# A hybrid SSD/attention block on one core: the store of the gated forms ten k steps later, the first gate/up pair in the common order, the first ring loads at their slots' release

## The chip, the cores and the metric

The kernel runs on one core of one Trainium2 chip. The metric is the device time of one execution in microseconds (us). The time before is 2273.95 us, the median of three runs (2269.09, 2274.33 and 2273.95).

## The reference

One transformer-like block on a sequence of 512 tokens, 2048 channels wide, all in fp32:

```python
u = rmsnorm(h, attn_norm_w)
z, xbc, dt_raw, q, kc, vc, ks, vs, kw, vw, gate_raw = jnp.split(u @ w_in, split_at, axis=-1)
y_ssd = ssd_mixer(z, xbc, dt_raw, conv_w, conv_b, dt_bias, a_log, d_skip, ssd_norm_w)
y_att = nsa_mixer(q, kc, vc, ks, vs, kw, vw, gate_raw, ...)
h = h + jnp.concatenate([y_ssd, y_att], axis=-1) @ w_out
v = rmsnorm(h, ffn_norm_w)
h = h + (jax.nn.silu(v @ w_gate) * (v @ w_up)) @ w_down
return rmsnorm(h, final_norm_w)
```

Only the line with `w_gate`, `w_up` and `w_down` matters here. `w_gate` and `w_up` are 2048 x 5632, `w_down` is 5632 x 2048.

## The kernel before

**Products.** Every fp32 operand is split into a high and a low part that TensorE reads as fp32r. ScalarE makes the high part (`a_hi`, L122: a copy that rounds), VectorE the low part (`lo`, L125: the operand less its high part). A product is then high by high, high by low and low by high. L134 is VectorE's plain addition, L128 its multiplication by two factors, L131 its multiplication, L281 a small operation of the norm.

**Gate and up.** The columns of `w_gate` and of `w_up` are worked in 22 pairs u = 0 to 21; one side of a pair is 256 columns of `w_gate` (side 0, gate) or of `w_up` (side 1, up). Each side is a 2x2 block product made with seven products in place of eight (Winograd's form of Strassen's scheme): M1 to M7. Their weight operands are the blocks 11, 12, 22 and the sums S1 = 21 + 22 and S3 = 21 + 11. S1 and S3 are made in memory: SyncE loads the first block, then GpSimd issues a load that adds the second one to it (L1109, `Z<-in_w_gate` and `Z<-in_w_up` on GpSimd's queue). M6 uses 11 with S1 added and M3 uses 12 with 11 added; VectorE makes these two sums just before the form is made (`sums`, L134). On the data's side M1, M2 and M6 use parts of v as they are, the others use T0 to T3, which are sums of the quarters of v, split into high and low parts in six pieces (`t_piece`).

**A step** is one of the seven products for one side: 8 k steps, each with a matmul of 512 columns and one of 256 (both L1168), so a side is 56 k steps and a pair 112. Each k step ends with `sch.tick()`, which lets the pending generators (evictions, silu, forms of the gated product) count down one; `yield n` in a generator means "go on n k steps from now". The high and low parts of a step's weights are issued two to three steps ahead of it (`prep(s.i + 2)`, `form(i + 1)`).

**Order and banks.** In pairs 1 to 20 the seven steps of a side come in the order SEQ = M1, M5, M6, M2, M7, M3, M4, gate whole and then up whole. M1, M6, M7 and M4 go into one PSUM bank, M5 and M3 into a second, M2 into a third (to which M1 is copied first, so that M2 adds to it). When a step ends, its bank is evicted: M1 (L1379), M6 (L1384), M2 (L1389), M5 (L1395) and M4 (L1411) by ScalarE, M7 and M3 by VectorE, which adds to an earlier eviction. So M6's eviction must be done before M7 may write. The banks have the names `ps_g`, `ps_s` and `ps_t` in turn.

In pairs 0 and 21 the two sides alternate step by step (`both_sides`). Pair 21 follows SEQ. Pair 0 follows M1, M2, M3 of both sides and then M6, M5, M7, M4 of both; M3's two sums (11 into S1's place and 12 plus 11) are made at once, and the pieces of T0 to T3 are made ahead of its steps 1 to 6.

**The gated product.** After M4 of up, `silu(gate) * up` of the pair stands in one buffer. `g_forms` (L1433 to L1455) makes its seven data forms for the down projection with their high and low parts: waits of 10, 4, 4 and 6 k steps lie between its pieces, and the last piece is the store of all seven (1.79 MB, L1454, `g_d<-A`) from ScalarE's queue. 24 k steps after M4 of up is the last k step of M6 of the next pair's gate side. ScalarE carries out its instructions in order, so what stands behind the store waits until the store is issued; the store is issued when the last low part is there.

**Down projection.** It walks over visits (a stretch of pairs for a block of output columns; L1172 to L1174 are its matmuls, L1524 and on its steps) and reads the stored forms through a ring of seven slots, whose memory is that of the parts of v and T0 to T3. Each slot is filled in two halves (forms 0 to 3 and 4 to 6, 1.0 MB and 0.77 MB) by `feed` (L1533 to L1553) with loads on ScalarE's queue (L1548, `u<-g_d`, `V<-g_d`, `T<-g_d`). A slot comes free when the last pair's up side is done with the step that reads it; `done[n - GRING, half]` holds that step's number for slot n. The first five early halves were issued at the third step behind the release (for slots 0 and 1 behind the release of the next slot).

The instructions are issued in the order of the program text from the first 16 steps of the output projection on; no scheduler moves them.

Of the kernel before, what the change touches and what calls it, by code (L numbers as in the profile page):

```python
# [10 lines left out]
AF = mybir.ActivationFunctionType  # L11
ALU = mybir.AluOpType
# [13 lines left out]
GRING = 7  # L26
# [17 lines left out]
M1, M2, M3, M4, M5, M6, M7 = range(1, 8)  # L44
V_OF = {M1: 0, M2: 1, M3: 2, M5: 3, M6: 4, M7: 5, M4: 6}
SEQ = [M1, M5, M6, M2, M7, M3, M4]
# [66 lines left out]
def body(ctx, tc, xT, w_in, w_out, w_gate, w_up, w_down, w1k, w1v, cols, rows, kst, out):  # L113
# [19 lines left out]
    def add(eng, o, a, b):  # L133
        eng.tensor_tensor(o, a, b, ALU.add)  # L134
# [1228 lines left out]
    def gu_after(u, side, got):  # L1363
        both = u in (0, NP - 1)

        def after(pr):
            def ev(p):
                wv = P2["A"][:, 12:28, :].rearrange("p (b a) t -> p b (a t)", b=4)
                if both:
                    wv = wv[:, 2 * side:2 * side + 2]  # L1370
                u2, m5 = wv[:, 0 if both else 1, :], wv[:, 1 if both else 3, :]
                ct = P2["CT"].rearrange("p (s c a) t -> p s c (a t)", s=2, c=2)
                c = ct[:, side].rearrange("p a t -> p (a t)")
                g = ct[:, 0].rearrange("p a t -> p (a t)")
                c4 = c.rearrange("p (a t) -> p a t", a=4)
                if pr == M1:
                    if u:
                        got["W"] = bank()
                    act.activation(got["W"] if u else u2, p, AF.Copy)  # L1379
                elif pr == M6:  # L1380
                    if u == 0:
                        add(dve, u2, got["W"], u2)
                        add(dve, c4[:, 0], u2[:, lo_h], u2[:, hi_h])
                    act.activation(u2, p, AF.Copy)  # L1384
                elif pr == M2:
                    if u and both:
                        fold(c4[:, 0], p)
                    elif u:
                        act.activation(wv[:, 0, :], p, AF.Copy)  # L1389
                elif pr == M5:  # L1390
                    if u == 0:
                        dve.tensor_tensor(m5, p, m5, ALU.subtract)
                        add(dve, u2, p, u2)
                    else:
                        act.activation(m5, p, AF.Copy)  # L1395
                elif pr == M7:
                    add(dve, m5, p, m5)
                    if u == 0:
                        add(dve, c4[:, 1:4:2], wv[:, :, lo_h], wv[:, :, hi_h])
                elif pr == M3:  # L1400
                    if u == 0:
                        act.activation(m5, p, AF.Copy)
                    else:
                        add(dve, u2, p, u2)
                        if both:
                            add(dve, c4[:, 1:4:2], wv[:, :, lo_h], wv[:, :, hi_h])
                elif pr == M4:
                    if both:
                        fold(c4[:, 2], p)
                    else:  # L1410
                        act.activation(wv[:, 2, :], p, AF.Copy)  # L1411
                        add(dve, c4, wv[:, :, lo_h], wv[:, :, hi_h])
                    if side == 0:
                        rr = rrow[:, None, :].to_broadcast([128, 2, 512])
                        c2 = ct[:, 0]
                        mul(dve, c2, c2, rr)
                        sch.add(silu(u, g, c2, rr, 0 if both else 10))
                    else:
                        sch.run_until(("r", u))
                        mul(dve, c, c, g)  # L1420
                        sch.add(g_forms(u))
            return ev
        return after
# [9 lines left out]
    def g_forms(u):  # L1433

        ct = P2["CT"].rearrange("p (s c a) t -> p s c (a t)", s=2, c=2)
        g = ct[:, 1]
        tg = ct[:, 0].rearrange("p a t -> p (a t)").rearrange("p (a t) -> p a t", a=4)
        sg = P2["ST"][:, 0:14, :].bitcast(F32R).rearrange("p (v s) t -> p v s t", s=2)
        yield 10
        a_hi(sg[:, 0, 0, :], g[:, 0, lo_h])  # L1440
        a_hi(sg[:, 1:3, 0, :], g[:, 1, :].rearrange("p (a t) -> p a t", a=2), scale=-1.0)
        gq = g.rearrange("p c (a t) -> p (c a) t", a=2)
        dve.tensor_tensor(tg[:, 1, :], gq[:, 1, :], gq[:, 0, :], ALU.subtract)
        add(dve, tg[:, 2, :], gq[:, 1, :], gq[:, 3, :])
        add(dve, tg[:, 0, :], tg[:, 1, :], gq[:, 3, :])
        dve.tensor_tensor(tg[:, 3, :], tg[:, 0, :], gq[:, 2, :], ALU.subtract)
        yield 4
        lo(dve, sg[:, 0, 1, :], g[:, 0, lo_h], sg[:, 0, 0, :])
        neg_lo(sg[:, 1:3, 1, :], g[:, 1, :].rearrange("p (a t) -> p a t", a=2), sg[:, 1:3, 0, :])
        a_hi(sg[:, 3:7, 0, :], tg)  # L1450
        yield 4
        lo(dve, sg[:, 3:7, 1, :], tg, sg[:, 3:7, 0, :])
        yield 6
        nc.scalar.dma_start(g_d[u].rearrange("v p n -> p v n"), f(sg).rearrange("p v s t -> p v (s t)"))  # L1454
        sch.flags.add(("g", u))  # L1455

    def start_ff(n):

        def before():
            if n == 0:  # L1460
                sch.run_until(*[("oa", c) for c in range(KD)])
                P2["T"].update({i: U[:, i - 2, 8:16, :].rearrange("p k (s t) -> p k s t", s=2) for i in (2, 3)})


                v = [P2["V0"], P2["VV"][:, 0], P2["VV"][:, 1]] + [P2["T"][i] for i in range(4)]
                P2["slot"] = [v[i] for i in V_SLOT]
                P2["turn"], P2["spare"] = 0, P2["SR"]
                P2["H"] = [x.rearrange("p (k a) t -> p k (a t)", a=2) for x in
                           [P2["A"][:, i:i + 10, :] for i in range(0, 70, 10)] + [P2["Z"][:, NZ2:NZ, :]]]
            else:  # L1470
                t_piece(*[(0, 1), (1, 1), (2, 0), (2, 1), (3, 0), (3, 1)][n - 1])
        return before

    r3 = rms_stats(acc2, D, rrow, "r3", rel=True)
# [13 lines left out]
    def both_sides(u, order, seq):  # L1488
        loads.extend(qs[u, int(a[0])][a[1:]] for a in order.split())
        bk = {i: gu_banks() for i in range(2)}  # L1490
        af = {i: gu_after(u, i, bk[i][0]) for i in range(2)}
        for n, (side, p) in enumerate(seq):
            ev = af[side](p)
            if u == 0 and n in (1, 4):
                ev = step_r3(ev)
            q = qs[u, side]
            b, sums = q["form"][p]
            if u == 0 and p in (M3, M6):
                sums = [(q["11"], q["S1"]), (q["12"], q["11"])] if p == M3 else ()
            if u and n == 0:  # L1500
                before = lambda: P2.update(spare=P2["ST"][:, 14:16, :])
            else:
                before = start_ff(n) if u == 0 and n < 7 else None
            s = Step(b, v_rhs(p), bk[side][1](p), after=ev, before=before, sums=sums,
                     wide=True)
            if (u, side) == (NP - 1, 1):
                n = V_SLOT.index(V_OF[p]) - GRING
                done[n, 0] = done[n, 1] = s.i

    done = {}  # L1510
    both_sides(0, "011 111 0S1 012 112 1S1 0S3 1S3 022 122", [(i, p) for p in (M1, M2, M3) for i in range(2)] +
               [(i, p) for p in (M6, M5, M7, M4) for i in range(2)])
    for u in range(1, NP - 1):
        for side in range(2):
            add_loads(qs[u, side])
# [15 lines left out]
    later = {}  # L1531

    def feed(i):  # L1533

        for half, r in ((0, slice(0, 4)), (1, slice(4, 7))):
            while nxt["ring", half] < NP:
                n = nxt["ring", half]
                at = max(done.get((n - GRING, half), i), later.get(n, 0))
                if n < 2 and half == 0:
                    at = done.get((n + 1 - GRING, 0), i)  # L1540
                if n < 5 and half == 1:
                    at = done.get((4 - GRING, 0), i) + n // 2
                if at + 3 > i:
                    break
                if n == NP - 1:
                    sch.run_until(("g", n))
                G[n] = P2["slot"][n % GRING]
                nc.scalar.dma_start(f(G[n][:, r]).rearrange("p v s t -> p v (s t)"),  # L1548
                                    g_d[n, r].rearrange("v p n -> p v n"))
                nxt["ring", half] += 1  # L1550
        if "H0" not in P2 and len(G) > 0 and not any(az.busy):
            load_h(0)
            P2["H0"] = True  # L1553
# [352 lines left out]
```

## Time and profile before

| | before |
|---|---|
| median of three runs | 2273.95 us |
| the profiled execution | 2275.06 us |
| its span, first to last instruction | 2273.3 us |
| its mean granted TensorE clock | 0.984 of full speed |
| first pair (0) | 893.02 to 939.20, 46.18 us |
| pairs 1 to 20 | 939.20 to 1752.77, 813.57 us |
| first visit of the down projection | 1791.99 to 1815.87, 23.88 us |

The profile names an instruction by its source line, engine, operation and the buffers that it writes and reads. PE is TensorE's matmuls, PEld its weight loads (beside the matmuls), DVE is VectorE, ACT is ScalarE, POOL is GpSimd, SP is SyncE; ACTq, POOLq and SPq are the DMAs that these issue. In a timeline row the first number is the start in us from the span's start, the second the duration; "x16" means sixteen alike in a row, and the brackets hold the idle time ahead of the row with what ended it. A row of the waits gives who waited for whom, the total in us, how often and the longest. A row of the DMA issues gives size and the time from issue to landing. Helpers record under one line: every high part is L122, every low part L125.

### The profile page before, as it was taken

How to read it: one execution, taken by the hardware profiler on the slowest of the kernel's cores; microseconds unless marked ns; L12 is line 12 of the kernel's file. 1: busy time of each engine (PE TensorE's matmuls, PEld its weight loads, DVE VectorE, ACT ScalarE, POOL GpSimd, SP SyncE). 2: the span in 40 equal slices, each digit the busy share in tenths (PEclk: the TensorE clock that was granted, in tenths of full speed). 3: DMA queues.
4: the chain of work that ended last, by engine and by line, in shares of the span. 5: the costliest groups of instructions: out<-in, count | busy, mean ns of one | idle time of the engine just before them, and what ended most of it. 6: DMA issues, size and time to landing. Idle time of an engine off the chain costs nothing. (4 is left out here: it accounts for less than half of the span.)

```text
span 2273.3 us, 35008 instructions
## 1 busy us (share of the span) xinstructions
PE 2177.7 (96%) x12904; PEld 1916.4 (84%) x12904; DVE 1822.6 (80%) x2858; ACT 1187.4 (52%) x1961; POOL 426.1 (19%) x433
## 2 busy tenths in 40 slices
PE   7999999999989989999999999999999899999996
PEld 5888888888877777888888888888888899999996
DVE  7699766688888667878888788887887798988897
ACT  4564446567666544655555555555555443333453
POOL 2011224223133224000000100001000121221222
PEclk8999999999989999999999999999999999999999
DMA  5222343222413265787878878788787969796974
GB/s 176 93 70 75 128 136 103 75 85 73 137 60 125 69 223 166 227 219 219 236 211 248 219 219 236 211 249 219 219 236 212 333 236 307 189 297 180 300 190 134
DMA packets 168555, 417.17 MB, mean 184 GB/s; under 512 B 16592, under 2 KB 23520, under 8 KB 168384
## 3 DMA queue, kind: packets, MB, share of 16 engines
q1 hardware_dynamic: 99776, 252.24, 33.7%
q0 software_dynamic: 25888, 76.72, 17.2%
q10 hardware_dynamic: 42720, 85.99, 10.5%
q8 instruction: 101, 1.65, 0.3%
q14 instruction: 70, 0.57, 0.1%
HBM read 353.80 MB, written 57.41 MB: 181 GB/s over the span
## 5 line engine op out<-in xcount | busy, mean ns | idle before, releaser
L122 ACT ACTIVATE R<-Z 128x1024 fp32r<-128x1024 f32 (+4 forms) x457 | 420.8, 934 | 442.7 <-DVE Z L134 315.0
L125 DVE TENSOR_TENSOR R<-Z,R 128x1024 fp32r<-128x1024 f32 (+4 forms) x363 | 393.6, 1092 | 41.1 <-ACT R L122 30.5
L232 PE MATMUL ps_g<-u,whi 128*128 128x512 f32 x720 | 286.1, 397 | 0.2 <-DVE h L131 0.2
L234 PE MATMUL ps_g<-u,wlo 128*128 128x512 f32 x720 | 284.4, 395 | 0.0
L233 PE MATMUL ps_g<-u,whi 128*128 128x512 f32 x720 | 283.9, 394 | 0.0
L1168 PE MATMUL ps_s<-u,R 128*128 128x512 f32 (+1 forms) x1152 | 253.4, 349 | 26.8 <-ACT A L1384 26.3
L1168 PEld LDWEIGHTS ps_s<-u,R 128*128 128x128 f32 x1152 | 186.6, 188 | 60.0 <-ACT A L1384 32.9
L125 DVE TENSOR_TENSOR wlo<-wraw,whi 128x512 fp32r<-128x512 f32 x196 | 151.3, 775 | 66.0 <-ACT whi L122 65.4
L122 ACT ACTIVATE whi<-wraw 128x512 fp32r<-128x512 f32 x196 | 122.6, 626 | 134.4 <-PE ps_g L233 89.7
L234 PEld LDWEIGHTS ps_g<-u,wlo 128*128 128x128 f32 x720 | 135.6, 188 | 27.1
L232 PEld LDWEIGHTS ps_g<-u,whi 128*128 128x128 f32 x720 | 135.9, 189 | 26.0 <-DVE h L131 0.5
L233 PEld LDWEIGHTS ps_g<-u,whi 128*128 128x128 f32 x720 | 135.8, 189 | 25.4
L1168 PE MATMUL ps_t<-u,R 128*128 128x512 f32 x592 | 132.5, 350 | 0.0
L134 DVE TENSOR_TENSOR A<-ps_g,A 128x512 f32<-128x512 f32 (+1 forms) x114 | 73.9, 655 | 73.1 <-PE ps_g L1168 39.1
L1168 PE MATMUL ps_g<-u,R 128*128 128x512 f32 (+1 forms) x600 | 131.5, 348 | 0.0
L1168 PE MATMUL ps_g<-T,R 128*128 128x512 f32 (+1 forms) x584 | 126.9, 348 | 0.0
L1168 PE MATMUL ps_s<-T,R 128*128 128x512 f32 (+1 forms) x552 | 123.9, 351 | 0.0
L1172 PE MATMUL ps_g<-u,R 128*128 128x256 f32 (+1 forms) x353 | 115.1, 326 | 9.0 <-ACT R L122 7.1
L122 ACT ACTIVATE R<-A 128x1024 fp32r<-128x1024 f32 (+3 forms) x79 | 74.7, 946 | 92.3 <-DVE A L134 65.2
L1168 PE MATMUL ps_s<-V,R 128*128 128x512 f32 (+1 forms) x568 | 122.7, 347 | 0.0
L125 DVE TENSOR_TENSOR E<-Z,R 128x1024 fp32r<-128x1024 f32 x94 | 114.6, 1219 | 9.4 <-ACT R L122 6.5
L1173 PE MATMUL ps_g<-u,R 128*128 128x256 f32 (+1 forms) x353 | 114.1, 323 | 0.0
(484 smaller groups left out, 5702.8 us busy)
## 6 DMA issues: line engine op xcount, KB each, us to landing
Z<-in_w_gate SPq DMA_DIRECT2D x95, 512.0 KB, 5.5
Z<-in_w_up SPq DMA_DIRECT2D x94, 512.0 KB, 5.1
wraw<-in_w_in SPq DMA_DIRECT2D x164, 256.0 KB, 2.6
g_d<-A ACTq DMA_DIRECT2D x22, 1792.0 KB, 13.9
Z<-in_w_gate POOLq DMA_DIRECT2D x39, 512.0 KB, 5.6
Z<-in_w_up POOLq DMA_DIRECT2D x38, 512.0 KB, 7.4
Z<-in_w_down SPq DMA_DIRECT2D x58, 320.0 KB, 5.4
Z<-in_w_down SPq DMA_DIRECT2D x40, 384.0 KB, 4.1
```

The costliest lines, as they stand in the source:

```text
L122: act.activation(dst, src, AF.Copy, scale=scale)
L125: eng.tensor_tensor(dst, src, f(hi), ALU.subtract)
L134: eng.tensor_tensor(o, a, b, ALU.add)
L232: pe.matmul(p, hi_t[i][:, j, :], ah, start=(k == 0), stop=False)
L233: pe.matmul(p, hi_t[i][:, j, :], al, start=False, stop=False)
L234: pe.matmul(p, lo_t[i][:, j, :], ah, start=False, stop=(k == u.nk - 1))
L1168: pe.matmul(o, w, x, start=start, stop=(k == n - 1 and o is q), skip_group_check=not fresh[0])
L1172: pe.matmul(q, h[:, k, :], ah, start=(k == 0), stop=False)
L1173: pe.matmul(q, h[:, k, :], al, start=False, stop=False)
```

## The change

Three edits. First, the store of the seven gated forms goes from 24 to 34 k steps after M4 of up (`yield 6` to `yield 16`). Second, pair 0 takes the order SEQ like the others, with its loads, the pieces of T0 to T3 (`PIECES`) and its evictions changed to suit: M1's eviction goes to a part of the result buffer, M2's eviction adds to it, and M6 and M3 get their one sum each, as in other pairs. Third, the early halves of ring slots 0 to 4 are issued at the first step behind the release of their memory, `done + 1`; the late halves are issued as before.

```diff
@@ evictions of gate and up (gu_after)
+                p1 = c[:, 256:768]
                 if pr == M1:
                     if u:
                         got["W"] = bank()
-                    act.activation(got["W"] if u else u2, p, AF.Copy)
+                    act.activation(got["W"] if u else p1, p, AF.Copy)
                 elif pr == M6:
-                    if u == 0:
-                        add(dve, u2, got["W"], u2)
-                        add(dve, c4[:, 0], u2[:, lo_h], u2[:, hi_h])
                     act.activation(u2, p, AF.Copy)
                 elif pr == M2:
-                    if u and both:
+                    if u == 0:
+                        add(dve, p1, p, p1)
+                        add(dve, c4[:, 0], p1[:, lo_h], p1[:, hi_h])
+                    elif both:
                         fold(c4[:, 0], p)
-                    elif u:
+                    else:
                         act.activation(wv[:, 0, :], p, AF.Copy)
                 elif pr == M5:
-                    if u == 0:
-                        dve.tensor_tensor(m5, p, m5, ALU.subtract)
-                        add(dve, u2, p, u2)
-                    else:
-                        act.activation(m5, p, AF.Copy)
+                    act.activation(m5, p, AF.Copy)
                 elif pr == M7:
                     add(dve, m5, p, m5)
...
@@ g_forms
         lo(dve, sg[:, 3:7, 1, :], tg, sg[:, 3:7, 0, :])
-        yield 6
+        yield 16
         nc.scalar.dma_start(g_d[u].rearrange("v p n -> p v n"), f(sg).rearrange("p v s t -> p v (s t)"))
         sch.flags.add(("g", u))
+
+    PIECES = {1: (1, 1), 4: (2, 0), 5: (2, 1), 7: (3, 0), 9: (3, 1)}
@@ start_ff
+                t_piece(0, 1)
             else:
-                t_piece(*[(0, 1), (1, 1), (2, 0), (2, 1), (3, 0), (3, 1)][n - 1])
+                t_piece(*PIECES[n])
@@ both_sides
-            if u == 0 and p in (M3, M6):
-                sums = [(q["11"], q["S1"]), (q["12"], q["11"])] if p == M3 else ()
...
-                before = start_ff(n) if u == 0 and n < 7 else None
+                before = start_ff(n) if u == 0 and (n == 0 or n in PIECES) else None
...
-    both_sides(0, "011 111 0S1 012 112 1S1 0S3 1S3 022 122", [(i, p) for p in (M1, M2, M3) for i in range(2)] +
-               [(i, p) for p in (M6, M5, M7, M4) for i in range(2)])
+    both_sides(0, "011 111 0S1 1S1 012 112 0S3 1S3 022 122", [(i, p) for p in SEQ for i in range(2)])
@@ feed
-                at = max(done.get((n - GRING, half), i), later.get(n, 0))
-                if n < 2 and half == 0:
-                    at = done.get((n + 1 - GRING, 0), i)
-                if n < 5 and half == 1:
-                    at = done.get((4 - GRING, 0), i) + n // 2
-                if at + 3 > i:
+                at = max(done.get((n - GRING, half), i), later.get(n, 0)) + 3
+                if n < 5:
+                    at = done.get((n - GRING, 0), i) + 1 if half == 0 else done.get((4 - GRING, 0), i) + 3 + n // 2
+                if at > i:
                     break
```

The numbers of the lines behind the edits shift: the evictions of M6, M2, M5 and M1 go from L1384, L1389, L1395 and L1379 to L1382, L1390, L1392 and L1380, the store from L1454 to L1446, the ring loads from L1548 to L1538.

The first place is ScalarE's instructions in the gate side of pair 11, from the eviction of M5 on; L1384 (L1382) is the eviction of M6, L1389 (L1390) that of M2, and `R<-Z` and `R<-A` are high parts of weights. Before:

```order
L1395 ACTIVATE A<-ps_g 128x512
L122 ACTIVATE R<-A 128x1024
L1454 DMA g_d<-A 128x7x512
L1384 ACTIVATE A<-ps_s 128x512
L122 ACTIVATE R<-Z 128x1024
L1389 ACTIVATE A<-ps_t 128x512
L122 ACTIVATE R<-Z 128x1024 x3
```

and of the change:

```order
L1392 ACTIVATE A<-ps_g 128x512
L122 ACTIVATE R<-Z 128x1024
L1382 ACTIVATE A<-ps_s 128x512
L122 ACTIVATE R<-Z 128x1024
L1390 ACTIVATE A<-ps_t 128x512
L122 ACTIVATE R<-Z 128x1024
L1446 DMA g_d<-A 128x7x512
L122 ACTIVATE R<-Z 128x1024 x2
```

The store has moved from ahead of M6's eviction to behind M2's and one more high part; two high parts, of later steps, follow it.

The second place is VectorE's instructions at the start of pair 0; `T_8314` is T0, the data operand of M5, `T_8315` is T1, that of M6, `E<-Z,R` and `R<-Z,R` are low parts of weights, `rst` is the norm's. Before:

```order
L128 SCALAR_TENSOR_TENSOR T_8314<-Z,T_8314 128x4x256
L134 TENSOR_TENSOR Z<-Z 128x1024 x2
L125 TENSOR_TENSOR R<-A,R 128x1024
L281 TENSOR_SCALAR rst<-ps_m 128x4
L131 TENSOR_TENSOR rst<-rst 128x4 x2
L125 TENSOR_TENSOR T_8315<-A,T_8315 128x4x256
L134 TENSOR_TENSOR Z<-Z 128x1024
L134 TENSOR_TENSOR A<-A,Z 128x1024
L125 TENSOR_TENSOR E<-Z,R 128x1024
```

and of the change:

```order
L125 TENSOR_TENSOR u<-A,u 128x2x256
L125 TENSOR_TENSOR T_8315<-A,T_8315 128x4x256
L134 TENSOR_TENSOR Z<-Z 128x1024
L125 TENSOR_TENSOR R<-Z,R 128x1024
L281 TENSOR_SCALAR rst<-ps_m 128x4
L131 TENSOR_TENSOR rst<-rst 128x4 x2
L134 TENSOR_TENSOR Z<-Z 128x1024
L125 TENSOR_TENSOR E<-Z,R 128x1024
```

One sum now stands ahead of each low part where two stood; T1's piece comes ahead of the first sum.

The third place is ScalarE's instructions in the last pair (21), between M1's evictions and M6's; `V_8321` and `T_8314` are ring slots. Before:

```order
L1395 ACTIVATE A<-ps_t 128x512
L122 ACTIVATE R<-Z 128x1024
L1395 ACTIVATE A<-ps_g 128x512
L122 ACTIVATE R<-Z 128x1024
L1384 ACTIVATE A<-ps_s 128x512
L122 ACTIVATE R<-Z 128x1024
L1384 ACTIVATE A<-ps_g 128x512
L1548 DMA V_8321<-g_d 128x4x512
```

and of the change:

```order
L1380 ACTIVATE ps_s<-ps_g 128x512
L1538 DMA V_8321<-g_d 128x4x512
L122 ACTIVATE R<-Z 128x1024
L1392 ACTIVATE A<-ps_t 128x512
L122 ACTIVATE R<-Z 128x1024
L1392 ACTIVATE A<-ps_g 128x512
L1538 DMA T_8314<-g_d 128x4x512
L122 ACTIVATE R<-A 128x1024
L1446 DMA g_d<-A 128x7x512
L1382 ACTIVATE A<-ps_s 128x512
```

The first ring load stands right behind M1's second eviction, four steps earlier, and the second right behind M5's; the store of pair 20 stands behind both of them.

More of the change, by code (lines that the diff above doesn't have):

```diff
@@ L1378, in ev @@
                         got["W"] = bank()
-                    act.activation(got["W"] if u else u2, p, AF.Copy)
+                    act.activation(got["W"] if u else p1, p, AF.Copy)
                 elif pr == M6:
-                    if u == 0:
-                        add(dve, u2, got["W"], u2)
-                        add(dve, c4[:, 0], u2[:, lo_h], u2[:, hi_h])
                     act.activation(u2, p, AF.Copy)
                 elif pr == M2:
-                    if u and both:
+                    if u == 0:
+                        add(dve, p1, p, p1)
+                        add(dve, c4[:, 0], p1[:, lo_h], p1[:, hi_h])
+                    elif both:
                         fold(c4[:, 0], p)
-                    elif u:
+                    else:
                         act.activation(wv[:, 0, :], p, AF.Copy)
                 elif pr == M5:
-                    if u == 0:
-                        dve.tensor_tensor(m5, p, m5, ALU.subtract)
-                        add(dve, u2, p, u2)
-                    else:
-                        act.activation(m5, p, AF.Copy)
+                    act.activation(m5, p, AF.Copy)
                 elif pr == M7:
                     add(dve, m5, p, m5)
-                    if u == 0:
+                elif pr == M3:
+                    add(dve, u2, p, u2)
+                    if both:
                         add(dve, c4[:, 1:4:2], wv[:, :, lo_h], wv[:, :, hi_h])
[L1400 to L1406, printed above, removed]
                 elif pr == M4:
```

## The prediction

> **What bounds the kernel now.** The page's first section comes first: which engine is near its limit.
>
> ```profile
> PE 2177.7 (96%) x12904; PEld 1916.4 (84%) x12904; DVE 1822.6 (80%) x2858; ACT 1187.4 (52%) x1961; POOL 426.1 (19%) x433
> ```
>
> TensorE (PE) is busy for 2177.7 of 2273.3 us, so about 96 us of it are idle. No edit of this change takes a matmul away; it can only win idle time. The profiled execution took 2275.06 us (1.8 us outside the span), 1.1 us over the median of the runs (2273.95). I sum against 2275.06. About 0.3%, 6.8 us, is what a measurement can tell from no change.
>
> Second, the busy time by stage. The columns are the stretch, its length, busy us of PE, PEld, DVE, ACT and POOL, the granted clock, the DMA share and GB/s.
>
> ```profile
> 893.02:939.20 46.18, 42.56 (x238) 36.69 (x236) 39.38 (x45) 25.80 (x31) 8.71 (x9) 0.96 0.66 176
> 910.50:913.94 3.44, 3.44 (x14) 2.96 (x13) 3.44 (x4) 2.55 (x3) 0.60 (x1) 0.50 0.45 151
> 939.20:1752.77 813.57, 787.26 (x4481) 684.42 (x4480) 661.89 (x682) 448.35 (x583) 69.54 (x81) 1.00 0.80 226
> 1712.23:1733.26 21.03, 19.82 (x113) 17.11 (x112) 17.62 (x21) 11.54 (x16) 1.73 (x2) 1.00 0.76 221
> 1733.26:1752.77 19.51, 19.51 (x113) 17.10 (x112) 14.61 (x14) 11.25 (x15) 2.16 (x3) 1.00 0.80 227
> 1791.99:1815.87 23.88, 17.36 (x107) 16.71 (x106) 18.90 (x26) 8.40 (x15) 7.11 (x5) 0.79 1.02 376
> ```
>
> These are the first pair, a piece of it at half clock, pairs 1 to 20, the gate side and the up side of pair 20, and the first visit of the down projection. The two sides hold the same 113 matmul records, yet gate takes 21.03 us and up 19.51: 1.52 us are lost on every gate side.
>
> Third, what PE waited for; the columns are total, times, longest.
>
> ```profile
> PE ps_s L1168 <- ACT A L1384: 26.3, 20, 2.4
> ...
> PE ps_t L1168 <- DVE E L125: 3.1, 1, 3.1
> PE ps_s L1172 <- DMA u<-g_d: 2.9, 1, 2.9
> ...
> PE ps_g L1172 <- DMA u<-g_d: 1.8, 1, 1.8
> ```
>
> The largest wait comes 20 times, once in each pair from 1 to 20, and ends with L1384, ScalarE's (ACT's) eviction of M6. Fourth, that place in the order of time, in one pair.
>
> ```profile
> 1396.66 1.07 ACT L122 ACTIVATE R<-Z 128x1024 fp32r<-128x1024 f32 x1 [0.59 <-DVE Z L134]
> 1398.87 0.37 ACTq L1454 DMA_DIRECT2D g_d<-A  x1
> 1399.28 0.60 ACT L1384 ACTIVATE A<-ps_s 128x512 f32<-128x512 f32 x1 [1.55 <-DVE A L125]
> ...
> 1397.62 1.22 DVE L125 TENSOR_TENSOR A<-A 128x1024 fp32r<-128x1024 f32 x1
> ...
> 1395.71 2.94 PE L1168 MATMUL ps_t<-u,R 128*128 128x512 f32 x16
> 1399.93 0.51 PE L1168 MATMUL ps_s<-u,R 128*128 128x512 f32 x1 [1.28 <-ACT A L1384]
> ```
>
> M7 writes the bank that M6's eviction reads. That eviction stands behind the store of the previous pair's forms on ACT's queue, and the store waits for VectorE's (DVE's) last low part (1397.62 + 1.22 = 1398.84). So ACT stands still for 1.55 us with a finished M6 before it, and M7 starts at 1399.93.
>
> **Part one, the store (pairs 1 to 20).** Without the store ahead of it the eviction follows the form: 1396.66 + 1.07 = 1397.73, plus 0.60 is 1398.33. A side without wait has 7 steps in 19.51 us, 2.787 each, so M7 is due at 1395.71 + 2.79 = 1398.50. The eviction makes it with 0.2 us to spare. The wait should go whole, but the next one stands close.
>
> The store's 34th k step is the second of M7: it now stands behind the evictions of M6 and M2 and two forms. Its data is 10 k steps (3.5 us) old by then, so it should wait for nothing, and its 0.37 us lie in ACT's idle time (448 of 814 us busy). Behind it wait forms of M3 and M4, two steps ahead of their use. The buffer that it reads is written again only 122 k steps after M4 (a pair is 112), 88 after the new issue, 31 us; the store lands in 13.6 (below).
>
> The bound of this part is 813.57 - 40 x 19.51 = 33.2 us. Two pieces may stay. Pair 1 waits 2.4 us, 1.1 more than the others, and I leave 0.8 there. The other is the up side's second wait:
>
> ```profile
> 1073.92 0.37 ACTq L1454 DMA_DIRECT2D g_d<-A  x1
> 1075.84 0.88 POOL L1109 DMA_DIRECT2D Z<-in_w_up  x1 [10.80 <-DMA Z<-in_w_up]
> 1088.59 1.06 ACT L122 ACTIVATE R<-Z 128x1024 fp32r<-128x1024 f32 x1 [1.58 <-DMA Z<-in_w_up]
> 1094.78 0.50 PE L1168 MATMUL ps_s<-u,R 128*128 128x512 f32 x1
> ...
> ACT R L122 <- DMA Z<-in_w_up: 6.5, 9, 1.6
> ...
> Z<-in_w_up POOLq DMA_DIRECT2D x1, 512.0 KB, 5.3
> ...
> Z<-in_w_up POOLq DMA_DIRECT2D x1, 512.0 KB, 12.7
> ...
> g_d<-A ACTq DMA_DIRECT2D x1, 1792.0 KB, 13.6
> ```
>
> The accumulating load of up's S3, issued 1.9 us after the store, lands in 12.7 us; the one before it, issued at 1064 with no store beside it, takes 5.3. ACT waits for it 9 times, 6.5 us in all. At 1.58 us of waiting PE loses only 0.14 (1094.78 against M2's 1091.86 + 2.78), so about 1.4 us of delay is free. But the load is anchored ahead of the stall that goes, and its user comes 1.5 us earlier: the free margin is spent. What is left is the nine waits, 6.5 us, less what the load wins because the store starts about level with it and no longer 1.9 us ahead. From 0 to 6.5 I take 2.4. **Part one: 33.2 - 0.8 - 2.4 = 30 us** (22 to 33).
>
> The Trainium skill says in "DMA: Bandwidth & Descriptors" (Issuing engines are not separate DMA queues) that transfers of all issuing engines run on the same 16 DMA engines and interleave. By it the later store still shares them with that load, and no order of issue shields it; this speaks against the change. The rows agree (12.7 against 5.3). If no time at all is won for the load, part one is 26 us and the total 2242.
>
> **Part two, the first pair.** 46.18 us stand against 14 steps x 2.787 = 39.02, plus the norm's small matmuls, about 1.5. So 5.7 us is the most that can be won. They are these:
>
> ```profile
> 903.17 2.82 PE L1168 MATMUL ps_s<-u,R 128*128 128x256 f32 x15 [0.50 <-DVE R L125]
> ...
> 909.35 0.38 PE L1168 MATMUL ps_t<-u,E 128*128 128x256 f32 x1 [3.12 <-DVE E L125]
> ...
> 906.93 1.22 DVE L134 TENSOR_TENSOR A<-A,Z 128x1024 f32<-128x1024 f32 x1
> 908.08 1.22 DVE L125 TENSOR_TENSOR E<-Z,R 128x1024 fp32r<-128x1024 f32 x1
> ...
> 896.49 1.20 POOL L1248 TENSOR_TENSOR A<-Z,A 128x256 f32<-128x256 f32 x1
> ```
>
> 3.12 us because M3 stood third and its two sums come ahead of its low part on DVE; 0.50; and 1.7 lost at half clock (3.44 us at 0.50), soon after the 3.12 us stall.
>
> In the new order M5 is third, without a sum, and M6 fifth with one. DVE's row: T1's piece waits for the subtraction on GpSimd (POOL) at 896.49 + 1.20, then ACT's high part (1.05), and ends near 900.0; one sum and M5-up's low part end at 902.5, where M5-up is due at 893.02 + 3 x 2.787 + 0.8 = 902.2: 0.4 us late. The norm's small operations, a sum and M6's low part end near 905.8, where M6 is due at 905.4: 0.4 more. After that DVE gains on PE. Up's S1 is now the fourth load, so it lands some 10 us before use. One late us and no half clock leave 4.5; I take **4 us**. The ends are 5.7, and -3.4 if one stall brings two half-clock windows (1.7 each).
>
> The Trainium skill, "TensorE: Matmul & The Clock Gate" (What's actually happening), gives the clock a free-running window of about 3.4 us after which an idle array runs at half rate. The 3.44 us at 0.50 agree. By it two waits of 0.4 us cost no window; were the half clock due to something else, this part would be 1.7 us smaller and the total 2239.7.
>
> **Part three, the first ring loads.** The first visit takes 23.88 us, of which 2.9 and 1.8 are waits for ring slots, with a clock of 0.79. The early half of slot 0 is now issued 4 steps earlier, of slots 1 to 4 two to four; the late halves stay.
>
> ```profile
> 1752.00:1772.00 20.00, 20.00 (x115) 17.33 (x114) 16.46 (x19) 12.62 (x17) 1.73 (x2) 1.00 0.72 176
> 1772.00:1792.00 20.00, 20.00 (x117) 17.54 (x116) 15.74 (x18) 6.67 (x9) 2.37 (x2) 1.00 1.04 389
> ...
> u<-g_d ACTq DMA_DIRECT2D x1, 1024.0 KB, 13.7
> ```
>
> The DMA engines are full from 1772 on and at 0.72 before. Two early halves (2.1 MB, 5.5 us at 389 GB/s) fit into the free share, so the later ones land about 5 us earlier; the slot that PE waits for, issued at 1782.7, took 13.7. The 2.9 us should go, the 1.8 perhaps. But DVE is busy 18.90 of the 23.88, so the visit can win at most 5.0. Zero is the other end; I take **3.4**. Each new issue now stands directly behind the eviction that frees its slot, so on ACT it adds 0.37 us each, inside 6.67 busy of 20. Should ACT block there, it is the forms of M3 and M4 that come late, with two steps of lead.
>
> Sum: 2275.06 - 30 - 4 - 3.4 = **2237.7**, say 2238. The forecast's own range, from the parts' ends: 2275.06 - 33.2 - 5.7 - 5.0 = 2231, to 2275.06 - 22 - 0 - 0 = 2253.
>
> **The rivals.**
> - The weight load takes the wait's place. In the ten pairs where up's S3 is latest, M7 of the up side loses the 1.53 us that gate won: 2238 + 15 = 2253; in all twenty, 2268. For it: margin 1.4 and loss 1.5 are equal, and store and load still overlap. Against it: 11 of 20 pairs show no wait at all, and the store's head start goes.
> - M6's eviction slips past its 0.2 us, since the sum and form ahead of it depend on DVE (1.55 us of its 39 are enough): 0.5 us a pair, 20 x 0.5 = 10, so 2248.
> - The edit doesn't do what it says, and M7 waits for something beside the store. Parts two and three alone give 2275.06 - 7.4 = 2267.7. Against: the store's wait and M7's wait match to the tenth.
> - Slower: the later store and up's S3 block each other. If that load lands in 15.0 us and not 12.7 (a ring load issued at 1784 took 15.0), it is 2.3 late, its user 1.53 early, with 1.1 of margin left in a mean pair: 2.75 lost against 1.53 won, 20 x 1.2 = 24 us, less 7.4: 2292. It decides once that load lands about 1.5 us later than now.
>
> ```profile
> V<-g_d ACTq DMA_DIRECT2D x1, 768.0 KB, 15.0
> ```
>
> **How the numbers follow.** Forecast 2238: 0.62. Weight load 2253: 0.20. Eviction 2248: 0.05. No effect 2267.7: 0.05. Slower 2292: 0.04. Below 2229, where all parts reach their bounds and more: 0.04. The range 2229 to 2260 leaves out the last three and the upper tail of the second, 0.17. Faster by over 0.3% (under 2267): all but the no-effect and slower cases and 0.01 of the weight loads, 0.90; within 0.3%: 0.06; slower: 0.04.
>
> **What would show it.** Part one: no PE wait on the M6 eviction (20 now), gate sides of 19.5 us, and ACT's wait ahead of the eviction gone. Wrong would be: PE waits in the up side's M7, ACT waits for in_w_up grown past 15 us in total. Part two: from the first gate matmul to pair 1 under 43 us, no clock of 0.50 in it. Part three: no wait for g_d in the first visit, DVE as what ends the waits left. The forecast fails if the pair's mean stays above 40 us (40.7 now).

## The result and the profile after

The changed kernel takes 2249.29 us, the median of four runs (2247.54 to 2254.77), against 2274.14 for the kernel before with its four runs. The ratio is 0.9898, with a 95% interval of 0.9878 to 0.9918: some 25 us less, where 36 were forecast. The time lies in the stated range, between the forecast (2238) and the first rival, the weight load (2253), and nearer to the rival. The profiled execution, the fastest of the four, took 2247.54 us, 27.5 less than the one of before.

First the page's first section after the change (busy us of each engine, share of the span):

```profile
span 2245.7 us, 35046 instructions
...
PE 2171.9 (97%) x12904; PEld 1913.6 (85%) x12904; DVE 1814.7 (81%) x2856; ACT 1182.8 (53%) x1961; POOL 425.0 (19%) x433
```

TensorE still idles 73.8 us of the span (95.6 before). Second, the stages, in the view by windows (length, busy PE, PEld, DVE, ACT, POOL, clock, DMA share, GB/s): the first pair, the gate side of pair 1, pairs 1 to 20, the gate side and the up side of pair 17, the first visit.

```profile
893.92:934.62 40.70, 40.70 (x237) 35.45 (x236) 34.89 (x40) 22.53 (x27) 7.71 (x9) 1.00 0.66 180
934.62:957.84 23.22, 20.33 (x114) 16.95 (x112) 21.34 (x25) 14.91 (x21) 1.72 (x2) 1.00 0.73 210
934.62:1728.82 794.20, 785.78 (x4481) 684.35 (x4480) 663.12 (x684) 445.94 (x586) 69.06 (x80) 1.00 0.82 233
1570.31:1589.88 19.57, 19.57 (x113) 17.14 (x112) 17.63 (x21) 11.43 (x16) 1.73 (x2) 1.00 0.78 211
1589.88:1610.57 20.69, 19.77 (x113) 17.10 (x112) 15.45 (x15) 10.68 (x15) 1.72 (x2) 1.00 0.86 243
1768.44:1790.11 21.67, 16.05 (x106) 15.44 (x105) 19.86 (x26) 8.30 (x15) 5.88 (x4) 0.84 0.86 316
```

The gate side, 21.03 before, is down to 19.57: its stall is gone. Now it is the up side that is long, 20.69 against 19.51. Third, the waits of PE and then those of ScalarE:

```profile
PE ps_s L1168 <- ACT A L1382: 6.1, 11, 0.9
...
PE ps_g L1172 <- DMA u<-g_d: 2.8, 1, 2.8
...
PE ps_g L1168 <- DVE R L125: 1.5, 1, 1.5
...
PE ps_s L1168 <- DVE E L125: 0.8, 1, 0.8
```

```profile
ACT R L122 <- DMA Z<-in_w_up: 32.8, 20, 2.5
...
ACT R L122 <- DMA Z<-in_w_gate: 6.6, 1, 6.6
```

M7's wait for M6's eviction is down from 26.3 us to 6.1, and ten of the eleven that are left stand in up sides. ScalarE's wait for the up side's S3 load has grown from 6.5 us to 32.8. These are the two signs of being wrong that the prediction named for part one.

For the balance each side is taken from the first matmul of its M1 to the first of the next. In us, from the two profiled executions:

| stage | before | after | won |
|---|---|---|---|
| up to the first pair | 893.02 | 893.92 | -0.90 |
| pair 0 | 46.18 | 40.70 | 5.48 |
| pair 1, gate and up | 22.18 + 19.52 | 23.22 + 19.98 | -1.50 |
| 19 gate sides, pairs 2 to 20 | 400.27 | 371.36 | 28.91 |
| 19 up sides, pairs 2 to 20 | 371.60 | 379.64 | -8.04 |
| pair 21 | 39.22 | 39.62 | -0.40 |
| first visit | 23.88 | 21.67 | 2.21 |
| the rest | 457.43 | 455.59 | 1.84 |

### The profile page after: what moved, and what is told of

Read it like the earlier page. It is cut to its first block, busy times and chain, and to the rows that moved or that the text cites. A ratio compares the mean times of both kernels' runs of the same rounds, so it can differ in the third digit from the quotient of the medians.

```text
span 2245.7 us, 35046 instructions
## 1 busy us (share of the span) xinstructions
PE 2171.9 (97%) x12904; PEld 1913.6 (85%) x12904; DVE 1814.7 (81%) x2856; ACT 1182.8 (53%) x1961; POOL 425.0 (19%) x433
## 5 line engine op out<-in xcount | busy, mean ns | idle before, releaser
L134 DVE TENSOR_TENSOR A<-ps_g,A 128x512 f32<-128x512 f32 (+1 forms) x114 | 73.9, 654 | 73.0 <-PE ps_g L1168 38.8
L1168 PE MATMUL ps_t<-u,R 128*128 128x512 f32 (+1 forms) x600 | 131.5, 348 | 0.0
L1168 PE MATMUL ps_g<-u,R 128*128 128x512 f32 x584 | 131.3, 349 | 0.0
```

Source lines behind the costliest of these rows:

```text
L1168: pe.matmul(o, w, x, start=start, stop=(k == n - 1 and o is q), skip_group_check=not fresh[0])
```

## The experiments

The theory behind them is the one called the load theory in the expectations. By it the accumulating load of up's S3 lands late because the store runs beside it, and ScalarE, waiting for it, holds up what stands behind. The table gives every run in us by stage, as above; "gate" and "up" are the sums over pairs 2 to 20, where a side without a wait (19.53) would make 371.1. Ratios are to the kernel before. The runs e1 to e4, e5 to e8 and e9 to e11 are three groups, each timed with the kernel before beside it, so across groups only ratios compare. e4 and e9 are the same kernel and came out at 0.9831 and 0.9854 (2235.13 and 2240.98 us); a difference of that size between groups tells nothing.

| run | ratio (95% interval) | pair 0 | pair 1 gate | gate | up | pair 21 | first visit |
|---|---|---|---|---|---|---|---|
| before | 1 | 46.18 | 22.18 | 400.27 | 371.60 | 39.22 | 23.88 |
| the change | 0.9898 (0.9878 to 0.9918) | 40.70 | 23.22 | 371.36 | 379.64 | 39.62 | 21.67 |
| e1 | 0.9908 (0.9893 to 0.9923) | 46.21 | 20.41 | 371.51 | 380.43 | 39.21 | 23.36 |
| e2 | 0.9992 (0.9982 to 1.0002) | 40.68 | 24.20 | 400.27 | 371.33 | 39.21 | 21.24 |
| e3 | 0.9836 (0.9821 to 0.9850) | 40.74 | 21.84 | 371.23 | 371.22 | 40.22 | 21.35 |
| e4 | 0.9831 (0.9816 to 0.9845) | 40.73 | 20.87 | 371.28 | 371.21 | 39.66 | 20.35 |
| e5 | 1.0005 (0.9996 to 1.0014) | 44.74 | 23.71 | 400.43 | 371.32 | 39.22 | 23.13 |
| e6 | 0.9884 (0.9870 to 0.9899) | 42.44 | 21.85 | 371.35 | 380.61 | 39.93 | 23.07 |
| e7 | 0.9836 (0.9821 to 0.9851) | 41.70 | 20.87 | 371.52 | 371.26 | 39.77 | 21.54 |
| e8 | 0.9864 (0.9847 to 0.9880) | 40.71 | 20.96 | 371.22 | 371.20 | 39.22 | 21.02 |
| e9 | 0.9854 (0.9839 to 0.9869) | 40.70 | 22.66 | 371.25 | 371.20 | 40.59 | 20.11 |
| e10 | 0.9854 (0.9835 to 0.9874) | 42.70 | 23.42 | 371.25 | 371.27 | 39.21 | 21.82 |
| e11 | 0.9861 (0.9845 to 0.9877) | 43.00 | 20.87 | 371.22 | 371.28 | 44.77 | 19.32 |

### e1: the store alone

```diff
--- the kernel before
-        yield 6
+        yield 16
         nc.scalar.dma_start(g_d[u]...
```

> The kernel before with the first edit alone (store at the 34th k step). Load theory (the up side's S3 load lands late beside the store, and its form holds up ScalarE's queue): gate sides of pairs 1 to 20 go to 19.5 us, up sides lose 8 to 10 us in all, so pairs 1 to 20 take 790 to 793 us instead of 813.57, the total falls by 20 to 23 us (ratio 0.990 to 0.991), ScalarE waits for in_w_up about 30 us (6.5 before). First pair 46.2 and first visit 23.9 stay. If the up side's loss in the changed kernel came from the other two edits, pairs 1 to 20 take 784 to 786 us and the ratio is 0.987.

The loss in the up sides is there with the first edit alone (380.43), and so is the whole gain in the gate sides. Pairs 1 to 20 took 793.68 us, 0.7 over the expected range, the ratio is as expected, and ScalarE waited:

```profile
ACT R L122 <- DMA Z<-in_w_up: 34.7, 18, 3.2
```

So it is the store edit itself that both wins the 29 us and gives back 9.

### e3: the store ten k steps later still

```diff
--- the changed kernel
-        yield 16
+        yield 26
         nc.scalar.dma_start(g_d[u]...
```

> The changed kernel with the store another ten k steps later (44th, last but four of M3). Load theory: the up side's S3 load, issued 13.2 us into the pair, is nearly through when the store starts at about 15 us; it lands in 5 to 8 us instead of 10 to 12, ScalarE waits for in_w_up under 8 us instead of 32.8, every up side is within 0.2 of 19.52, pairs 1 to 20 take 784 to 788 us instead of 794.2, the total is 7 to 10 us below the changed kernel (2240; ratio to before 0.985). Rival, the load is anchored too late whatever runs beside it: pairs 1 to 20 stay at 794, the total at 2249. Second rival, the store now slows the next gate side's loads as much: up sides become 19.5 but gate sides 20 and more, total 2245 to 2255.

The up sides lost nothing any more (371.22), the gate sides neither (371.23), and the total was 2236.96 us, a little below what was expected. The timeline of pair 17 in e3, then from the DMA issues the time of that load in e3 and, behind it, in the changed kernel, then ScalarE's wait in e3:

```profile
1572.05 0.86 POOL L1109 DMA_DIRECT2D Z<-in_w_up  x1 [11.49 <-DMA Z<-in_w_up]
...
1573.28 1.07 ACT L122 ACTIVATE R<-Z 128x1024 fp32r<-128x1024 f32 x1 [0.90 <-ACT R L122]
1573.36 0.37 ACTq L1446 DMA_DIRECT2D g_d<-A  x1
```

```profile
Z<-in_w_up POOLq DMA_DIRECT2D x1, 512.0 KB, 9.7
```

```profile
Z<-in_w_up POOLq DMA_DIRECT2D x1, 512.0 KB, 12.4
```

```profile
ACT R L122 <- DMA Z<-in_w_up: 5.9, 6, 3.2
```

The store now starts 1.3 us behind the load and not 1.6 ahead. The load still takes 9.7 us, more than the 5 to 8 expected, but 2.7 less than in the changed kernel, and that is enough: ScalarE's wait falls from 32.8 to 5.9 us. Pair 17 is a long case; over pairs 2 to 20 this load takes 9.6 us in the mean in e3 (8.3 to 10.8), 11.6 in the changed kernel (10.8 to 12.4) and 11.4 before (10.8 to 12.7). The rival that the load is anchored too late, whatever runs beside it, falls.

### e4: silu ahead of the form

```diff
--- the changed kernel
+        def go():
+            act.activation(g[:, 0:512], g[:, 0:512], AF.Silu)
+            act.activation(g[:, 512:1024], g[:, 512:1024], AF.Silu, scale=-1.0)
+        if n:
+            P2["silu"] = go
         yield n
...
                 Step(b, v_rhs(p), bk(p), after=af(p), sums=sums, wide=True,
+                     before=(lambda: P2.pop("silu")()) if (side, p) == (1, M5) else None)
```

> The changed kernel with the two silu activations issued ahead of the form of up's S3 on ScalarE and not behind it. If the late load costs its time through what stands behind its form on ScalarE (silu, then VectorE's product, M3's sum and form, M6's eviction): ScalarE still waits 15 to 33 us for in_w_up, but up sides fall to 19.5 to 19.7, pairs 1 to 20 take 784 to 788 us, the total 2239 to 2243 (ratio to before 0.985). Rival, VectorE's own load or M6's eviction makes M7 late: up sides and the total stay as in the changed kernel (794.2 and 2249).

How a late load reaches TensorE is read from the changed kernel's timeline, in the up side of pair 17:

```profile
1595.95 1.06 ACT L122 ACTIVATE R<-Z 128x1024 fp32r<-128x1024 f32 x1 [2.51 <-DMA Z<-in_w_up]
...
1597.44 0.61 ACT L1420 ACTIVATE A<-A 128x512 f32<-128x512 f32 x1
...
1598.09 1.23 DVE L131 TENSOR_TENSOR A<-A,rrow 128x1024 f32<-128x1024 f32 x1 [2.50 <-ACT A L1420]
...
1599.23 1.22 DVE L134 TENSOR_TENSOR Z<-Z 128x1024 f32<-128x1024 f32 x1
...
1600.54 1.06 ACT L122 ACTIVATE R<-Z 128x1024 fp32r<-128x1024 f32 x1 [2.00 <-DVE Z L134]
1601.51 0.57 ACT L1382 ACTIVATE A<-ps_s 128x512 f32<-128x512 f32 x1
...
1602.14 0.61 PE L1168 MATMUL ps_s<-u,R 128*128 128x512 f32 x2 [0.92 <-ACT A L1382]
```

M7 doesn't wait for its own weights. S3's form (1595.95) keeps the silu (L1419, L1420) of the same pair behind it on ScalarE; VectorE's product (L131) waits for the silu, M3's sum (L134) stands behind that product, M3's form (1600.54) behind the sum, and M6's eviction (1601.51) behind M3's form. In e4 the same place, four instructions of ScalarE's timeline in the up side of pair 17, and then its wait, read:

```profile
1581.16 0.61 ACT L1420 ACTIVATE A<-A 128x512 f32<-128x512 f32 x1
1583.09 1.07 ACT L122 ACTIVATE R<-Z 128x1024 fp32r<-128x1024 f32 x1 [1.32 <-DMA Z<-in_w_up]
...
1585.22 1.07 ACT L122 ACTIVATE R<-Z 128x1024 fp32r<-128x1024 f32 x1 [0.58 <-DVE Z L134]
1586.19 0.57 ACT L1382 ACTIVATE A<-ps_s 128x512 f32<-128x512 f32 x1
```

```profile
ACT R L122 <- DMA Z<-in_w_up: 14.3, 16, 2.0
```

ScalarE still waits for the load 16 times, 14.3 us in all (a little under the 15 to 33 expected; the silu's two activations now fill part of the wait), but the wait no longer reaches TensorE, which has no wait left in the up sides: they took 371.21 us, and the total was 2235.13, 4 us under the expected range. The rival that VectorE or the eviction itself is late falls.

### e6: the store right behind M6's eviction

```diff
--- the changed kernel
-        yield 16
+        yield 7
         nc.scalar.dma_start(g_d[u]...
```

> The changed kernel with the store at the 25th k step, the first one behind M6's eviction, 3.1 us earlier than in the change. By the load theory the store then runs 4.6 us ahead of up's S3 load and still beside it for some 9 us: that load lands a little sooner (9 to 11 us), up sides of pairs 2 to 20 lose 2 to 7 us in all (8.5 in the changed kernel), gate sides stay at 19.5, pairs 1 to 20 take 786 to 793 us, total 2239 to 2248. If only a store behind the load helps: 794 and 2249 as in the changed kernel, or worse. If the store's wait for the low part still stands in a queue that matters: gate sides over 19.8.

Neither sooner nor cheaper: gate and up sides as in the changed kernel (371.35, 380.61), and the total was 2247.08 us. The timelines say why, of the changed kernel and of e6, in the gate side of pair 17:

```profile
1580.69 1.22 DVE L125 TENSOR_TENSOR A<-A 128x1024 fp32r<-128x1024 f32 x1
...
1581.94 0.37 ACTq L1446 DMA_DIRECT2D g_d<-A  x1
1582.13 0.59 ACT L1390 ACTIVATE A<-ps_t 128x512 f32<-128x512 f32 x1
...
1583.49 0.86 POOL L1109 DMA_DIRECT2D Z<-in_w_up  x1 [10.04 <-DMA Z<-in_w_up]
```

```profile
1580.35 1.22 DVE L125 TENSOR_TENSOR A<-A 128x1024 fp32r<-128x1024 f32 x1
...
1581.60 0.37 ACTq L1446 DMA_DIRECT2D g_d<-A  x1
```

In both the store goes out 0.03 us after its last low part is ready (1580.69 + 1.22 = 1581.91; 1580.35 + 1.22 = 1581.57). The gate sides begin at 1570.31 and 1569.95, so it starts 11.63 and 11.65 us into the side; before the change it was 11.81 in the pair that the prediction shows (1073.92, side from 1062.11). These three are the latest of their profiles: over pairs 2 to 20 the store starts about 11.5 us into the side before, in the change and in e6 alike, 0.03 to 0.05 us after its low part. The expectation's 3.1 us of head start couldn't come about. In the changed kernel the issue even comes ahead of the start of M2's eviction (1582.13), which stands before the store in the program. From the 24th to the 34th k step the number moves the store in ScalarE's order only. In time it moves in e3, where it stands behind a high part that starts at 1573.28, well after the low part (14.33 us into the side).

### e7: both remedies

The silu as in e4 and `yield 26` as in e3.

> Both remedies together (silu ahead of the form, store at the 44th k step). Each of them alone brought the up sides to 19.53 and 19.52, so by the load theory nothing is left to win in pairs 2 to 20: 742.5 us there, pairs 1 to 20 at 782 to 784, total 2232 to 2238, not distinguishable from either alone. If they removed two different losses: 4 us or more below both (under 2231).

2236.35 us, with gate and up sides of 742.8: the two remove the same loss.

### e2: the first pair alone

The kernel before with the second edit only.

> The kernel before with the second edit alone (first pair in the common order). If the first pair's shorter time makes pair 1's S1 load late (load theory): first pair 40.7 us, and TensorE waits 1.3 to 1.7 us for a low part at M5 of pair 1, whose gate side grows from 22.18 to 23.5 to 24.5; the total falls by 3 to 4.5 us (ratio 0.998 to 0.9987). If pair 1's new waits came from the later store: gate side of pair 1 stays 22.2, the total falls by 5.5 us (0.9976).

The first pair takes 40.68 us, but pair 1's gate side 24.20, together 64.88 against 68.36: 3.5 us won in the profiled executions. By the ratio it is 1.8 us, with an interval from 4.1 less to 0.5 more, so the gain in the total isn't clear of the noise. By windows:

```profile
891.28:931.96 40.68, 40.68 (x238) 35.45 (x237) 36.18 (x43) 24.32 (x29) 7.79 (x9) 1.00 0.67 184
931.96:956.16 24.20, 21.62 (x113) 18.33 (x112) 19.75 (x23) 13.14 (x18) 1.72 (x2) 0.93 0.79 227
```

The side's length was as the load theory had it, but not its cause, so the agreement is luck: PE waited nothing at M5 and 0.2 us at M6, and the rest came from the clock of 0.93 after the store's stall (2.39 us). In the changed kernel it is ScalarE that waits for pair 1's S1 load; VectorE waits for an eviction of the first pair behind that form, and M5 of pair 1 follows:

```profile
933.88 1.06 ACT L122 ACTIVATE R<-Z 128x1024 fp32r<-128x1024 f32 x1 [6.63 <-DMA Z<-in_w_gate]
...
935.25 0.43 DVE L134 TENSOR_TENSOR A<-ps_s,A 128x256 f32<-128x256 f32 x1 [2.26 <-ACT A L1360]
...
939.26 0.62 PE L1168 MATMUL ps_g<-T,R 128*128 128x256 f32 x2 [1.47 <-DVE R L125]
```

### e8: pair 1's S1 first

```diff
--- e4's kernel
-            add_loads(qs[u, side])
+            add_loads(qs[u, side], "S1 11 12 S3 22" if (u, side) == (1, 0) else "11 S1 12 S3 22")
```

> The kernel with silu ahead of the form, and pair 1's gate loads in the order S1, 11 and not 11, S1. If pair 1's lost time comes from its S1 load (ScalarE waited 2.9 to 6.6 us for it ahead of the first pair's last evictions): that wait falls under 1.5 us, the gate side of pair 1 to 20.2 or less (20.87 in e4, 23.22 in the changed kernel), total 0 to 2 us below e4. If the wait is not what holds pair 1: wait gone, gate side unchanged at 20.9 or more.

A miss: ScalarE's wait for a gate load in that stretch was 4.4 us (2.9 in e4), not less, and the side took 20.96. The total was 2241.60 us, over e4 but not over e9, which is e4's kernel again; by stages the difference of the profiled executions lies behind the first visit, where this edit does nothing. Nor would a gain of 2 us on this side have told much: e4 and e9 have 20.87 and 22.66 there. Of the 1.4 us over 19.53, which would be free of waits, 0.9 are two waits of TensorE: 0.27 at M6 for a low part and 0.65 at M7 for M6's eviction. What holds these was not settled.

### e5, e9, e10 and e11: the ring loads

e5 is the kernel before with the third edit only. e9 is e4's kernel again, e10 is e4's kernel with the ring loads as before, and e11 is e4's kernel with two late halves sooner:

```diff
--- e4's kernel
-                    at = done.get((n - GRING, 0), i) + 1 if half == 0 else done.get((4 - GRING, 0), i) + 3 + n // 2
+                    at = done.get((n - GRING, 0), i) + 1 if half == 0 or n < 2 else done.get((4 - GRING, 0), i) + 3 + n // 2
```

> The kernel before with the third edit alone (early ring halves at their slots' release). If the ring loads save about 2 us whatever comes ahead of them: first visit 21.3 to 22.2 us (23.88 before, 23.36 with the store edit alone), the wait for a ring slot at its first step (2.9 before) gone, pairs 1 to 20 at 813.6, total 1.5 to 3 us lower (ratio 0.9987 to 0.9993). If the first visit gained only because the pairs ahead of it end earlier: 23.5 to 24 us and ratio 1.000.

> The same kernel as e4, timed again as the mark for the two beside it: total 2232 to 2240 (e4: 2235.13), first visit of the down projection 20 to 22 us.

> e4's kernel with the ring loads as in the kernel before. If the ring edit saves 2 us (as the first visits of the changed kernel, e3 and e4 against before and e1 have it): first visit 23.3 to 24 us, total 1.5 to 3 us above e9. If it is worth nothing in the end (e5: ratio 1.0005; from the first visit's start to the end 481.3, 479.6 and 481.2 us without the edit, 477.3, 479.8, 478.8, 483.7, 479.2, 479.0 and 484.7 with it): total within 1 us of e9.

> e4's kernel with the late halves of ring slots 0 and 1 issued right behind their early halves, some 25 us sooner. If the first visit waits because ScalarE's queue holds the ring load of a u slot until V's late half has landed (issue 1773.09 against landing 1773.08 in the changed kernel, 1795.90 against 1795.88 in e5): that load is issued 8 us or more earlier, the wait for u<-g_d of 2.8 us goes, the first visit falls to 18.5 to 20.5 us, total 1 to 3 us below e9. If the DMA engines' share (full from the last pair's second half on) or VectorE sets the first visit: 21 to 22 us again, total unchanged.

Alone the edit is worth nothing that can be measured: 1.0005, with an interval from 0.9 us less to 3.2 more. e9 and e10 have the same ratio, 0.9854. Their medians, 2240.98 and 2243.53 us, lie 2.55 apart, which by e10's expectation would speak for the edit, but e10's four runs go from 2236.09 to 2245.49 and its first visit took 21.82 us and not 23.3 or more; beside the silu ahead of the form, 2 us either way can't be told. (e9's median is 0.98 over the upper end expected.) The first visit's length isn't fixed by the edit either: without it 23.88, 23.36, 21.24 and 21.82, with it 20.1 to 23.1. Taken from pair 21's start to the span's end, the old ring loads need 518.8 to 522.6 us (before, e1, e2 and e10, mean 520.6), the new ones 516.9 to 523.9 (the change, e3 to e9, mean 520.1): 0.5 us apart in a scatter of several. Part of what they win may be paid in pair 21: it lasts 39.21 or 39.22 us in all four profiles with the old loads, and 39.22 to 40.59 in the eight with the new ones.

In the changed kernel the visit waits for a later load, of which the timeline and the DMA issues show:

```profile
1763.48 0.37 ACTq L1538 DMA_DIRECT2D V<-g_d  x1
...
1773.09 0.37 ACTq L1538 DMA_DIRECT2D u<-g_d  x1
```

```profile
V<-g_d ACTq DMA_DIRECT2D x1, 768.0 KB, 9.6
```

The load of the u slot is issued at the moment at which V's late half lands (1763.48 + 9.6 = 1773.08), and PE waits 2.8 us for it. The trace's record of the issue names what it waits for: semaphore 116, the one that V's late half counts up as it lands. In pair 21 it is the same: ScalarE stands still for 7.5 us, and the u load that it then issues (1762.41) comes right behind a wait for semaphore 114, on which the load of T issued at 1745.98 lands at 1762.33. e11 takes V's late half out of the way, and there is no wait for `g_d` in its first visit (19.32 us). But the loads now weigh on the last pair. By windows, pair 21 and the first visit of e9 and then of e11, and behind them ScalarE's largest wait in pair 21 of each:

```profile
1717.09:1757.68 40.59, 39.52 (x226) 34.16 (x224) 30.70 (x36) 19.07 (x26) 4.86 (x4) 1.00 0.94 305
1757.68:1777.79 20.11, 14.73 (x106) 14.12 (x105) 18.56 (x26) 8.30 (x15) 4.29 (x3) 0.92 0.89 329
```

```profile
1717.47:1762.24 44.77, 41.33 (x225) 35.26 (x224) 31.27 (x36) 18.95 (x26) 4.86 (x4) 0.96 0.98 318
1762.24:1781.56 19.32, 15.69 (x107) 15.28 (x105) 18.46 (x25) 7.76 (x14) 6.31 (x4) 0.82 0.72 247
```

```profile
ACT R L122 <- issue: 7.7, 2, 7.4
```

```profile
ACT R L122 <- issue: 13.0, 2, 7.3
```

The visit wins 0.8 us and the pair loses 4.2, and the total is that of e9 (2241.31 and 2240.98 us). In pair 21 ScalarE stands still at its own ring loads for 13.0 us and not 7.7, TensorE waits 2.0 and 1.5 us for low parts, the DMA share is at 0.98 and the clock at 0.96; which of these weighs most was not tried, and neither was a kernel whose ring loads don't share semaphores.

## Why the prediction was right, and where it was not

The time lies in the stated range and moved the way that was forecast, but part one alone fell out of its own range: pairs 1 to 20 won 19.4 us (813.57 less 794.20), where 30 were forecast and 22 was the lower end. The total stayed inside the range because part two came out 1.5 us above its forecast in this profile, because 0.9 us came in stretches that no edit touches, and because the stated range reached beyond the parts' ends; that much is luck.

**The bound and the stall: right.** The store in front of M6's eviction cost 1.52 us on each gate side. It is gone on all 19 sides of pairs 2 to 20 (28.91 us), and the margin of 0.2 us for the eviction held: these gate sides have no wait left. e1 shows it with the first edit alone.

**What part one leaves: the term that failed.** The forecast kept 2.4 us for the up side's second wait and took the rest away "because the store starts about level with it and no longer 1.9 us ahead". The step behind that was that the store's data would be ten k steps old at the 34th k step. It was not: the last low part ends 11.5 us into the side whatever the number says. The prediction's own rows had it (1398.84, with M2 at 1395.71 and three steps of 2.787 ahead of it), and 34 k steps are only 11.8 us. So the store starts when it did before, 1.6 us ahead of the load in the pair shown and 1.9 before. The load was issued 13.1 us into the pair in the mean and landed at 24.7 (13.3 and 24.8 before), since what releases it is the load of its first block and not the stall, while its user came about 1.5 us earlier. The term measured 8.5 us in pairs 2 to 20 (379.64 less 371.1) and 0.5 in pair 1, more than the 6.5 that the forecast had as its upper end. It counted only the nine pairs in which ScalarE had waited; of the twelve up sides that lost time, six had no such wait before.

The Trainium skill's rule that the forecast weighed is that transfers of all issuing engines share the 16 DMA engines ("DMA: Bandwidth & Descriptors", Issuing engines are not separate DMA queues). The trace agrees with the rule: the load takes 11.6 us in the mean with the store starting ahead of it and 9.6 with the store behind it. e3 and e6 show that the overlap in time counts, and the place in the queue doesn't. The forecast's sum for no time won at the load was 2242.

**The first rival, the weight load: its mechanism held, its price was smaller.** It put the loss at ten pairs of 1.53 us, 15 us. Twelve up sides of pairs 2 to 20 lost 0.2 to 1.2. The 1.4 us of free delay that the forecast read from one pair held nearly: in all twelve the loss is ScalarE's wait for the load less 1.3 us, from 1.51 us of wait and 0.24 lost to 2.51 and 1.16. The way is not the one named: not M7's weights, but the silu behind them in ScalarE's order (e4).

**Part two: right in size, by another way.** Forecast 4 us. The first pair won 5.48, close to the bound of 5.7, with none of the two waits of 0.4 us that the working had. That is in part luck: of the nine other profiles of the new order five have no wait over 0.1 us, but e7 has 0.8 us of waits, and e6, e10 and e11 have 1.5 to 2.0, mostly at up's M5, which the working had as the first to be late; the ten take 41.4 us in the mean. Pair 1, where the forecast left 0.8 us, gave back some: gate and up together take 43.20 us, 1.5 more than before and than in e1, which has the later store without the new order (41.70 and 41.74). e2 puts the net at 3.5 in its profile, and its total leaves it open.

**Part three: not borne out.** Forecast 3.4 us; the changed profile shows 2.21 less in the first visit and 0.40 more in pair 21, but e5 and e10 show no difference in the total that can be measured. The first slots' loads do land early, as the forecast had it; the visit then waits 2.8 us for a load that the edit doesn't move and 2.8 us for VectorE. What the forecast named as a caveat, that ScalarE might block at the new issues, came about: 7.5 us in pair 21, of which TensorE felt 0.1.

**The other rivals.** The eviction slipping past its margin, the edit without effect, and the store and S3's load blocking each other for a loss: none came. The last needed the load to take about 1.5 us longer than before; over pairs 2 to 20 it took 11.6 us against 11.4.

**The faster version.** The change with the silu ahead of S3's form (e4, e9) has ratios of 0.9831 and 0.9854, with the store at the 44th k step (e3) 0.9836, both (e7) 0.9836; the change alone 0.9898. Either of the two is enough.

## What to carry to other kernels

A stall that is taken away brings every later user forward, but not the transfers that are issued ahead of it: their margin shrinks by just the time won, and the next wait should be priced with that in full. An instruction that waits for a transfer on an in-order engine should have nothing behind it on which other engines depend; moving two short activations ahead of it won as much here as moving the transfer (e4 and e3). And before a store is counted as later or earlier, look at when its data is ready: a number of steps in the program moves its place in the order, and its time only if the data was there.

## What was not expected of the hardware

The same stall doesn't always cost half clock. In pair 0 of the old order TensorE waits 3.1 and 0.5 us in before, e1 and e5 alike; by windows the first is at a clock of 0.96 and the last at 1.00, and they take 46.18 and 44.74 us:

```profile
890.96:935.70 44.74, 41.09 (x238) 35.40 (x236) 39.40 (x45) 25.69 (x31) 7.81 (x9) 1.00 0.64 182
```

And the 2.4 us stall of pair 1 left the clock at 1.00 in before and brought it to 0.93 in e5, which has the same work up to there, and in e2. The gate side of pair 1 in before and then in e5:

```profile
939.20:961.38 22.18, 19.80 (x114) 17.04 (x112) 19.31 (x23) 12.73 (x18) 1.72 (x2) 1.00 0.72 210
```

```profile
935.70:959.41 23.71, 21.33 (x113) 18.33 (x112) 19.29 (x23) 12.71 (x18) 1.72 (x2) 0.93 0.71 209
```

TensorE is busy 1.5 us longer for the same matmuls. Each of the two profiles paid once, before in pair 0 and e5 in pair 1 (68.36 and 68.45 us together). So such a price comes and goes from run to run with the same work, and a sum should hold it as a range.
